# Two-layer hybrid decoder trunk: the buffers laid out anew in on-chip memory

## The chip, the cores and the metric

The kernel runs on one core of a Trainium2 chip. The core has five engines that run side by side and meet at semaphores: TensorE (matmuls, "PE" in the profile, its weight loads "PEld"), VectorE ("DVE"), ScalarE ("ACT"), GpSimd ("POOL") and SyncE ("SP"), which here issues all transfers between the main memory (HBM) and the on-chip memory (SBUF). SBUF has 128 partitions; a buffer is a range of bytes that starts at the same address in each of them. Matmuls write to a second memory, PSUM. The metric is the device time of one execution in microseconds.

## What is computed

Two layers over 256 tokens of width 1024, in float32. Each has a mixer (stick-breaking attention and softmax attention with rotary, 8 heads of 64 each, gated and merged) and a SwiGLU part of inner width 2816, each followed by a LayerNorm over alpha x plus the part's output:

```python
for l in range(DEPTH):                                        # DEPTH = 2
    proj = x @ w_in[l]                                        # 1024 -> 5120
    q_sb, k_sb, v_sb, q_mb, k_mb, v_mb, g_sb, g_mb = jnp.split(proj, cuts, axis=-1)
    o_sb = stick_breaking_attention(heads(q_sb, 8), heads(k_sb, 8), heads(v_sb, 8))
    o_mb = moba_attention(partial_rope(heads(q_mb, 8), pos), partial_rope(heads(k_mb, 8), pos), heads(v_mb, 8))
    merged = jax.nn.sigmoid(g_sb) * (merge_heads(o_sb) @ w_branch_sb[l]) \
           + jax.nn.sigmoid(g_mb) * (merge_heads(o_mb) @ w_branch_moba[l])
    x = layer_norm(ALPHA * x + merged @ w_out[l], ln_mix_g[l], ln_mix_b[l])
    ffn = (jax.nn.silu(x @ w_ffn_gate[l]) * (x @ w_ffn_up[l])) @ w_ffn_down[l]
    x = layer_norm(ALPHA * x + ffn, ln_ffn_g[l], ln_ffn_b[l])
```

## The kernel before

**Numbers in two parts.** Every operand of a matmul is held as two float32r parts, hi (rounded) and lo (the rest). A product a b is three matmuls, hi hi, hi lo and lo hi (`mm3`, whose matmuls all stand at line 275 in `mm`). A matmul has a stationary operand, 128 columns that a weight load puts into the array, and a moving operand that streams past it.

**Weights** come in 244 granules of 128 partitions x 1024 float32 (`WeightStream`): a load of 512 KB from SP into one of four buffers `raw` (L119), a cast by ScalarE into `whi` (helper line L48), and a subtraction by VectorE into `wlo` (L53). There are ten buffers each of whi and wlo; a granule's split starts when a pair is free. `Weave` writes one program order for all engines, in which these splits and the attention, rotary and norm steps stand between the matmuls of the main line.

**The stages of a layer** and their names in the profile: `pv`, `pq` (in layer 1 together `pvq`), `pk`, `pu` are projections with tokens on the partitions (`tok_major`): xT is stationary and 512 weight columns move. `pqk` (q and k of stick-breaking, four tiles of 2 x 24 matmuls), `pg` (gates, 8 x 48) and `pf` (SwiGLU from the fifth chunk on, 18 x 48) are feature-major (`feat_major`): 128 weight columns are stationary and all 256 tokens of xT move. `pb` is the branch projection with the attention's outputs `osb` and `omb` moving, `pw` the output projection, `pft` the first SwiGLU chunks in tok_major, `pd` the down projection (512 weight columns move, the activations `h` are stationary); in layer 1 its second half of tokens is `pe`, partly with 256 columns.

**xT** is the transposed x, in two parts xT_hi and xT_lo of 8 KB per partition; each norm writes it anew. x itself is `xs`, two tiles of 4 KB.

**Buffers** come from pools, laid one behind the other in SBUF in the order in which the pools are opened: `const`, `wpool` (raw, whi, wlo), `acts` (15 units of 4 KB), `work` (attention and small activations), `small`. Tiles of a few bytes take 32.

Of the kernel before, what the change touches and what calls it, by code (L numbers as in the profile page):

```python
# [7 lines left out]
F32 = mybir.dt.float32  # L8
F32R = mybir.dt.float32r
# [5 lines left out]
P = 128  # L15
DEPTH = 2
D = 1024
S = 256
KC = D // P
# [15 lines left out]
class Weave:  # L35
    """Program order: the main line of projections, with side lines (attention, norms,
    rotary, weight splits) woven in. Every engine takes its instructions in program order,
    so each is emitted about when its operands are there, by an estimate of the time at
    which each engine gets through what it has been given. A side line yields the time
    at which it goes on; on the tensor engine's clock."""  # L40

# [40 lines left out]
    def start(self, gen):  # L82
        """A side line whose first stage comes now."""
        side = self.add(gen)
        if not self.busy:
            self._step(side)
        return side
# [9 lines left out]
class WeightStream:  # L97
    """Weight granules [128, 1024]: loaded in float32, then split exactly into
    two float32r parts (hi = rounded, lo = the rest) for the tensor engine."""

# [24 lines left out]
    def line(self):  # L125
        """The side line: a granule at a time, as far as the buffers allow."""
        nc, weave = self.nc, self.weave
        while self.split < self.total:
            g = self.split
            ahead = g - self.current  # L130
            if g > self.limit:
                yield weave.t + 0.1
                continue
            if ahead >= LEAD and max(weave.dve_t, weave.act_t) > weave.t + BACKLOG:
                yield weave.t + 0.2
                continue
            self.load(g + NRAW)
            if ahead > 0:
                yield self.there[g]
            hi, lo = (self.pool.tile([P, GCOLS], F32R, tag=n, name=f"{n}{g}", bufs=NSPLIT)  # L140
                      for n in ("whi", "wlo"))
            t = self.raw.pop(g)
            n = GCOLS // len(self._pieces(g))
            for sl in self._pieces(g):
                e = weave.act(self.there[g], n, nc.scalar.copy, hi[:, sl], t[:, sl])
            if g - self.current > 0:
                yield e
            for sl in self._pieces(g):
                e = weave.dve(e, n, nc.vector.tensor_sub, lo[:, sl], t[:, sl], hi[:, sl].bitcast(F32))
            self.parts[g], self.ready[g] = (hi, lo), e  # L150
            self.split += 1
            self.load(g + 1 + NRAW)

    def allow(self, g):
        """Granule g's buffers are free from here on."""
        self.limit = max(self.limit, min(g, self.total - 1))
# [7 lines left out]


NRAW = 4
NSPLIT = 10
# [12 lines left out]
def hybrid_trunk_kernel(ctx: ExitStack, tc: tile.TileContext, w, xT_in, x_in, ln_in,  # L180
                        ident_in, mask_in, rope_in, out):
    nc = tc.nc

    const = ctx.enter_context(tc.tile_pool(name="const", bufs=1))
    wpool = ctx.enter_context(tc.tile_pool(name="wpool", bufs=1))
    acts = ctx.enter_context(tc.tile_pool(name="acts", bufs=15))
    work = ctx.enter_context(tc.tile_pool(name="work", bufs=3))
    small = ctx.enter_context(tc.tile_pool(name="small", bufs=2))
    psM = ctx.enter_context(tc.tile_pool(name="psM", bufs=2, space=PSUM))
# [22 lines left out]

# [1 line left out]
    xT_raw = [unit(f"xT_raw{t}", [P, KC, P]) for t in range(2)]  # L214
    ident = const.tile([P, P], F32, name="ident")
    rope = const.tile([P, 2, 2, ROPE], F32, name="rope")
    xs = [const.tile([P, D], F32, name=f"x{t}") for t in range(2)]
    xT_hi = const.tile([P, KC, S], F32R, name="xT_hi")
    xT_lo = const.tile([P, KC, S], F32R, name="xT_lo")
    mask = const.tile([P, 2, P], F32, name="mask")  # L220
# [4 lines left out]
    nc.vector.memset(zero, 0.0)  # L225
    nc.vector.memset(mhalf, -0.5)
    nc.scalar.activation(warm, zero, AF.Sigmoid)
    # The tensor engine's clock rises after some microseconds of work: give it zeros meanwhile.
    idle = unit("idle", [P, 512], F32R)
# [42 lines left out]

# [1 line left out]
    def mm(o, a, b, start, stop):  # L274
# [30 lines left out]
    def tok_major(o, g, t, first, last, k0):  # L305
        """o[tokens of t, 512] += x @ granule g ([2 kc, 512])."""
        hi, lo = ws.take(g)
        hi = hi.rearrange("p (k c) -> p k c", k=2)
        lo = lo.rearrange("p (k c) -> p k c", k=2)
        for k in range(2):  # L310
            ts = slice(t * P, (t + 1) * P)
            mm3(o, xT_hi[:, k0 + k, ts], xT_lo[:, k0 + k, ts], hi[:, k, :], lo[:, k, :],
                first and k == 0, last and k == 1)

    def both_tokens(name, g0, put):
        """All tokens of x @ granules g0..g0+3; put(tokens, bank) takes each half."""
        acc = [bankM(f"{name}{t}", [P, WIDTH]) for t in range(2)]
        order = ((0, 0), (1, 0), (0, 1), (1, 1), (0, 2), (0, 3)) if g0 == 0 else \
            ((0, 0), (0, 1), (0, 2), (1, 0), (1, 1), (0, 3))
        for t, k in order + ((1, 2), (1, 3)):  # L320
            tok_major(acc[t], g0 + k, t, k == 0, k == 3, 2 * k)
            if t == 1:
                ws.allow(g0 + k + NSPLIT)
            if k == 3:
                put(t, acc[t])

    def feat_major(o, g):
        """o[128 columns, 256 tokens] = (x @ granule g)^T, g [8 kc, 128 columns]."""
        hi, lo = ws.take(g)
        hi = hi.rearrange("p (k c) -> p k c", k=KC)  # L330
# [5 lines left out]
    def token_out(o, g, t, s_hi, s_lo, first, last):  # L336
        """o[tokens of t, 1024] += s^T @ granule g ([1 kc, 1024]); o: (first column, bank) ..."""
        hi, lo = ws.take(g)
# [6 lines left out]

    # Per head, q is stacked as [hi; lo] over the 128 rows and each part of k is there twice,
    # so that q k^T = q_stack (k_hi twice) + q_stack (k_lo twice).
    def stack_q(qs, src, n, c, e):
        """qs[head] [128, ...] from src [2 heads x 64, ...]; the second head is [lo; hi]."""
        for h, (a, b) in enumerate(ROWS):  # L350
# [20 lines left out]
    def rope_line(name, ps, t, put):  # L371
        """Token-major q or k (8 heads x 64) -> rotary -> transposed, handed to put."""
        tmp = work.tile([P, 8, DH], F32, tag="T", name=f"{name}_tok{t}")
# [22 lines left out]
    def scores(s, q, kh, kl, m):  # L396
        """Scores of both heads of a pair: columns 0:128 = (q0, k0), 128:384 = (q1, k0 k1),
        with the causal mask m added to the diagonal blocks."""
        for h in range(2):
# [12 lines left out]
    def weighted(name, p, wt, v, oT, e):  # L412
        """oT[:, p] = (wt @ v)^T for both heads of pair p."""
        yield e + MARGIN
# [93 lines left out]
    def scale_shift(e, x, cols, sub, op, scale, g, b, e_scale):  # L508
        """x <- ((x op sub) g) scale + b; yields each piece of columns as it is done."""
        for c in cols:  # L510
# [7 lines left out]
    def norm_line(name, t, junk, gb):  # L518
        """x_t <- LN(alpha x_t + ps) g + b, and its transpose into xT (split)."""
        x = xs[t]  # L520
# [26 lines left out]
    def last_norm(name, t, banks, gb, down):  # L547
        """The output's tokens: LN(alpha x_t + sum) g + b, blocks of columns in turn."""
        x = xs[t]
# [24 lines left out]

# [1 line left out]
    norms = []  # L576
    for l in range(DEPTH):
        G = l * NG_LAYER
        L = f"l{l}"

        # v of stick-breaking and q of MoBA: tokens 0..127 first
        v_sb = pair_tiles(L + "vsb", [P, 2, WIDTH])
# [28 lines left out]

        # Each pair of stick-breaking heads starts with its q and k; k and v of MoBA and the
        # first gates come between, MoBA's heads after the last sigmoid of stick-breaking, and
        # the gates' sigmoids after the last exponential of MoBA.
        o_sb = pair_tiles(L + "osb", [P, NPAIR, S])
# [47 lines left out]

        # branch projections and the gated merge, feature-major
        gb = load_gb(l, 0)
# [20 lines left out]

        # output projection: tokens 0..127 first
        norms = []
# [7 lines left out]

        # SwiGLU, first chunks token-major (tokens 0..127 first)
        h_t = [pair_tiles(f"{L}h{i}", [P, 4, S]) for i in range((NFC + 3) // 4)]
# [47 lines left out]

        # down projection: the last granules' tokens 0..127 first
        gb = load_gb(l, 1)
# [108 lines left out]
```

## Time and profile before

| | us |
|---|---|
| time, median of 3 runs (753.32 to 755.79) | 753.6 |
| span of the profiled execution | 747.6 |
| TensorE busy (98% of the span) | 735.1 |
| VectorE busy | 529.9 |
| ScalarE busy | 421.8 |
| GpSimd busy | 13.4 |

The span reaches from the first to the last instruction of the profiled execution; the median is 6.0 us longer than it. TensorE's busy time counts overlapping matmuls once, so it tells that matmuls follow each other nearly always, and not how fast. Transfers move 136.31 MB at a mean of 182 GB/s. The pace of the matmuls is read from the chain of work: the length of an unbroken piece, divided by the matmuls in it.

### The profile page before, as it was taken

What the parts mean: (1) busy time and instruction counts of PE and PEld (TensorE: products, weight loads), DVE (VectorE), ACT (ScalarE), POOL (GpSimd) and SP (SyncE); (2) the same over time, 40 slices, a digit from 0 to 9 for tenths busy, and PEclk for the clock granted to TensorE, in tenths of its full rate; (3) what the DMA queues carried; (4) which work ended last, traced back from release to release, by engine and by line L of the source; (5) the groups of instructions that cost most, each with busy time, mean ns of one, the idle gap of its engine ahead of it and who ended that gap; (6) DMA issues with size and microseconds to landing.
All of it is one profiled execution on the core that took longest, in us unless ns stands there. A gap on an engine that the chain in (4) does not pass through costs nothing.

```text
span 747.6 us, 12689 instructions
## 1 busy us (share of the span) xinstructions
PE 735.1 (98%) x5049; PEld 675.5 (90%) x5049; DVE 529.9 (71%) x772; ACT 421.8 (56%) x655; POOL 13.4 (2%) x20
## 2 busy tenths in 40 slices
PE   8999999999999999999999999999999999999996
PEld 5888999998799999988888889999987999999885
DVE  6897878696886666644488878886768866665416
ACT  6788867744565445433267877777435654554300
POOL 0000000000000000000000000000010000000001
PEclk9999999999999999999999999999999999999999
DMA  8864724554586565676168445345635865657501
GB/s 292 284 217 151 221 93 153 176 199 167 178 265 227 181 194 182 198 241 194 60 196 258 146 162 177 108 145 198 210 113 183 277 201 194 196 185 246 166 1 56
DMA packets 39082, 136.31 MB, mean 182 GB/s; under 512 B 4464, under 2 KB 6000, under 8 KB 39024
## 3 DMA queue, kind: packets, MB, share of 16 engines
q1 hardware_dynamic: 39024, 135.51, 55.6%
q8 instruction: 39, 0.64, 0.3%
q14 instruction: 19, 0.16, 0.1%
HBM read 134.45 MB, written 1.05 MB: 181 GB/s over the span
## 4 chain that ended last, share of the span: by engine, by line
PE 84%; DVE 6%; ACT 3%; DMA 3%; issue 2%; POOL 1%; SPq 0%; POOLq 0%; DVEq 0%; ACTq 0%
PE l0pf L275 14%; PE l1pf L275 13%; PE l0pd L275 8%; PE l1pg L275 6%; PE l0pg L275 6%; PE l1pe L275 4%; PE l1pd L275 4%; PE l1pb L275 3%; PE l0pb L275 3%; PE l1pvq L275 3%; DMA raw<-in_w_dram 3%; PE l1pw L275 2%; PE l0pw L275 2%; PE l1pqk L275 2%; DVE wlo L53 2%
## 5 line engine op out<-in xcount | busy, mean ns | idle before, releaser
L53 DVE TENSOR_TENSOR wlo<-raw,whi 128x1024 fp32r<-128x1024 f32 (+1 forms) x245 | 296.8, 1219 | 93.0 <-ACT whi L48 89.5
L48 ACT CAST whi<-raw 128x1024 fp32r<-128x1024 f32 (+1 forms) x245 | 254.1, 1046 | 86.7 <-PE l0pd L275 22.6
L275 PE MATMUL l0pf<-xT_hi,whi 128*128 128x256 f32 x288 | 81.0, 281 | 0.0
L275 PE MATMUL l0pf<-xT_lo,whi 128*128 128x256 f32 x288 | 80.9, 281 | 0.0
L275 PE MATMUL l0pf<-xT_hi,wlo 128*128 128x256 f32 x288 | 80.9, 281 | 0.0
L275 PE MATMUL l1pf<-xT_hi,whi 128*128 128x256 f32 x288 | 79.6, 276 | 0.0
L275 PE MATMUL l1pf<-xT_lo,whi 128*128 128x256 f32 x288 | 79.5, 276 | 0.0
L275 PE MATMUL l1pf<-xT_hi,wlo 128*128 128x256 f32 x288 | 79.5, 276 | 0.0
L275 PEld LDWEIGHTS l0pf<-xT_hi,wlo 128*128 128x128 f32 x288 | 55.3, 192 | 0.0
L275 PEld LDWEIGHTS l0pf<-xT_lo,whi 128*128 128x128 f32 x288 | 54.1, 188 | 0.0
L275 PEld LDWEIGHTS l1pf<-xT_lo,whi 128*128 128x128 f32 x288 | 54.1, 188 | 0.0
L275 PEld LDWEIGHTS l0pf<-xT_hi,whi 128*128 128x128 f32 x288 | 54.1, 188 | 0.0
L275 PEld LDWEIGHTS l1pf<-xT_hi,whi 128*128 128x128 f32 x288 | 54.1, 188 | 0.0
L275 PEld LDWEIGHTS l1pf<-xT_hi,wlo 128*128 128x128 f32 x288 | 54.1, 188 | 0.0
L275 PE MATMUL l0pg<-xT_hi,whi 128*128 128x256 f32 x128 | 35.9, 281 | 0.0
L275 PE MATMUL l1pg<-xT_hi,whi 128*128 128x256 f32 x128 | 35.9, 281 | 0.0
L275 PE MATMUL l0pg<-xT_lo,whi 128*128 128x256 f32 x128 | 35.5, 277 | 0.0
L275 PE MATMUL l1pg<-xT_lo,whi 128*128 128x256 f32 x128 | 35.5, 277 | 0.0
L275 PE MATMUL l1pg<-xT_hi,wlo 128*128 128x256 f32 x128 | 35.4, 277 | 0.0
L275 PE MATMUL l0pg<-xT_hi,wlo 128*128 128x256 f32 x128 | 35.4, 277 | 0.0
L275 PE MATMUL l0pd<-whi,l0h_hi 128*128 128x512 f32 x88 | 34.4, 391 | 0.0
L275 PE MATMUL l0pd<-whi,l0h_lo 128*128 128x512 f32 x88 | 34.3, 389 | 0.0
(379 smaller groups left out, 1821.1 us busy)
## 6 DMA issues: line engine op xcount, KB each, us to landing
raw<-in_w_dram SPq DMA_DIRECT2D x243, 512.0 KB, 4.1
ln<-in_ln_dram SPq DMA_DIRECT2D x8, 512.0 KB, 7.3
xT_raw<-in_xT_dram SPq DMA_DIRECT2D x8, 128.0 KB, 5.0
x<-in_x_dram SPq DMA_DIRECT2D x2, 512.0 KB, 6.4
out_dram<-x SPq DMA_DIRECT2D x3, 256.0 KB, 2.1
raw<-in_w_dram SPq DMA_DIRECT2D x2, 256.0 KB, 3.7
out_dram<-x SPq DMA_DIRECT2D x2, 128.0 KB, 2.0
mask<-in_mask_dram SPq DMA_DIRECT2D x1, 128.0 KB, 3.2
```

Source lines behind the costliest of these rows:

```text
L48: f(*args, **kw)
L53: f(*args, **kw)
L275: nc.tensor.matmul(o, a, b, start=start, stop=stop)
```

## The change

The pools are opened in another order, and a filler stands behind the small tiles. `const` keeps ident, rope, mask and the two constants; behind it come `small` and a pool `fill` with one tile `page` of 576 bytes; then `big` with xs, xT_hi and xT_lo; then wpool, acts and work as before. `page` has to be written once, so GpSimd sets one element of it. Comments and docstrings became blank lines.

```diff
+FILL = 144
@@
     const = ctx.enter_context(tc.tile_pool(name="const", bufs=1))
+    small = ctx.enter_context(tc.tile_pool(name="small", bufs=2))
+    fill = ctx.enter_context(tc.tile_pool(name="fill", bufs=1))
+    big = ctx.enter_context(tc.tile_pool(name="big", bufs=1))
     wpool = ctx.enter_context(tc.tile_pool(name="wpool", bufs=1))
     acts = ctx.enter_context(tc.tile_pool(name="acts", bufs=15))
     work = ctx.enter_context(tc.tile_pool(name="work", bufs=3))
-    small = ctx.enter_context(tc.tile_pool(name="small", bufs=2))
@@
-    xs = [const.tile([P, D], F32, name=f"x{t}") for t in range(2)]
-    xT_hi = const.tile([P, KC, S], F32R, name="xT_hi")
-    xT_lo = const.tile([P, KC, S], F32R, name="xT_lo")
+    xs = [big.tile([P, D], F32, name=f"x{t}") for t in range(2)]
+    xT_hi = big.tile([P, KC, S], F32R, name="xT_hi")
+    xT_lo = big.tile([P, KC, S], F32R, name="xT_lo")
+    page = fill.tile([P, FILL], F32, name="page")
@@
     nc.vector.memset(mhalf, -0.5)
+    nc.gpsimd.memset(page[:, :1], 0.0)
     nc.scalar.activation(warm, zero, AF.Sigmoid)
```

The built programs place the buffers so. The first 16,512 bytes are taken by the system and its constants in both; before, x0 starts at 16,512 + 512 (ident) + 256 (rope) = 17,280, and after, the small tiles and the filler end at 20,480, where x0 starts.

| buffers | first address before | offset modulo 512 before | first address after | offset modulo 512 after |
|---|---|---|---|---|
| ident, rope | 16,512 | 128 | 16,512 | 128 |
| x0, x1 | 17,280 | 384 | 20,480 | 0 |
| xT_hi, xT_lo | 25,472 | 384 | 28,672 | 0 |
| raw (4), whi (10), wlo (10) | 42,944 | 448 | 45,056 | 0 |
| units: v, q and k of MoBA, osb, omb, gates, m, h, ln | 141,248 | 448 | 143,360 | 0 |
| work: q and k of stick-breaking, ph, pl, T | 202,688 | 448 | 204,800 | 0 |

All sizes from x0 on are multiples of 1024 bytes, so the offset holds for each buffer of a row. Between a weight's start and xT's lie, modulo 512, 64 bytes before and none after; all other pairs of weights and activations keep a difference of 0.

With buffer numbers left out, the instructions of TensorE, VectorE, ScalarE and SP stand in the same order with the same waits. GpSimd has one more. Its first instructions in the program before, from the system's constants to the first norm:

```order
L843 MEMSET const-uint8-127 128x1
L853 UNCONDITIONAL_BRANCH
L58 ISA
L58 TENSOR_SCALAR l0a_ve_2113<-l0a_ve_2113 128x1
L58 TENSOR_TENSOR l0a_ve_2113<-l0a_ve_2113,mhalf 128x1
```

And the same place in the changed program:

```order
L850 MEMSET const-uint8-127 128x1
L860 UNCONDITIONAL_BRANCH
L233 MEMSET page 128x1
L58 ISA
L58 TENSOR_SCALAR l0a_ve_2121<-l0a_ve_2121 128x1
L58 TENSOR_TENSOR l0a_ve_2121<-l0a_ve_2121,mhalf 128x1
```

Only the memset of `page` came in; nothing on GpSimd stands ahead of it but the system's own start.

## Rows read from the trace of the kernel before

**Rows 1.** The page's first part: busy time, share of the span, instructions of each engine.
```profile
PE 735.1 (98%) x5049; PEld 675.5 (90%) x5049; DVE 529.9 (71%) x772; ACT 421.8 (56%) x655; POOL 13.4 (2%) x20
```

**Rows 2.** The page's fourth part: the chain that ended last, by engine.
```profile
PE 84%; DVE 6%; ACT 3%; DMA 3%; issue 2%; POOL 1%; SPq 0%; POOLq 0%; DVEq 0%; ACTq 0%
```

**Rows 3.** That chain in order of time: start us, length us, what, instructions.
```profile
4.47 5.78 DMA raw<-in_w_dram
10.55 4.64 DMA raw<-in_w_dram
...
77.56 5.44 PE l0pg L275 x48
...
83.92 5.65 PE l0pqk L275 x48
...
99.30 2.83 PE l0pg L275 x24
...
143.10 23.02 PE l0pb L275 x192
...
209.47 3.44 PE l0pft L275 x15
...
215.20 99.64 PE l0pf L275 x846
314.84 55.08 PE l0pd L275 x243
...
583.38 95.90 PE l1pf L275 x846
```

**Rows 4.** Busy time by stretch: stretch, length, engines with instructions, PEclk, DMA share, GB/s.
```profile
143.10:166.12 23.02, 23.02 (x194) 23.02 (x193) 18.89 (x30) 13.95 (x22) 0.00 (x0) 1.00 0.62 221
215.20:314.84 99.64, 99.64 (x847) 99.64 (x847) 66.05 (x90) 50.50 (x72) 0.00 (x0) 1.00 0.62 203
...
583.38:679.28 95.90, 95.90 (x848) 95.90 (x847) 65.88 (x90) 50.52 (x72) 0.00 (x0) 1.00 0.65 210
```

**Rows 5.** Groups of weight loads: line engine op names shapes xcount | busy us, mean ns.
```profile
L275 PEld LDWEIGHTS l1pf<-xT_hi,wlo 128*128 128x128 f32 x288 | 54.1, 188 | 0.0
...
L275 PEld LDWEIGHTS l0pb<-l0omb_hi,whi 128*128 128x128 f32 x32 | 6.1, 192 | 0.0
```

**Rows 6.** TensorE in time, entry of l0pb and 256 columns of l1pe: start, length.
```profile
142.94 0.28 PE L275 MATMUL l0pb<-l0osb_hi,whi 128*128 128x256 f32 x1
...
143.17 0.28 PE L275 MATMUL l0pb<-l0osb_hi,wlo 128*128 128x256 f32 x1
...
144.00 0.28 PE L275 MATMUL l0pb<-l0osb_hi,whi 128*128 128x256 f32 x1
...
144.36 0.28 PE L275 MATMUL l0pb<-l0omb_hi,whi 128*128 128x256 f32 x1
...
734.73 0.28 PE L275 MATMUL l1pe<-whi,l1h_hi 128*128 128x256 f32 x1
...
735.09 0.28 PE L275 MATMUL l1pe<-whi,l1h_hi 128*128 128x256 f32 x1
```

**Rows 7.** TensorE in time, start of the long stretch of l1pf.
```profile
583.34 0.28 PE L275 MATMUL l1pf<-xT_lo,whi 128*128 128x256 f32 x1
...
583.69 0.28 PE L275 MATMUL l1pf<-xT_lo,whi 128*128 128x256 f32 x1
...
584.49 0.28 PE L275 MATMUL l1pf<-xT_hi,wlo 128*128 128x256 f32 x1
```

**Rows 8.** Groups on GpSimd: xcount | busy us, mean ns | idle before us, releaser.
```profile
L58 POOL TENSOR_SCALAR l0a_ve<-l0a_ve 128x1 f32<-128x1 f32 x2 | 1.5, 748 | 190.0 <-ACT l0pw L48 190.0
...
L843 POOL MEMSET const-float32-0.0<- 128x1 f32 x1 | 0.1, 99 | 0.2 <-issue 0.2
```

**Rows 9.** Groups on VectorE: two steps of a norm on x.
```profile
L53 DVE SCALAR_TENSOR_TENSOR x<-x,l0a_ve,ln 128x512 f32<-128x512 f32 x4 | 2.8, 749 | 0.9 <-POOL l0a_ve L58 0.9
...
L53 DVE SCALAR_TENSOR_TENSOR x<-x,l0pw 128x512 f32<-128x512 f32 x4 | 2.6, 683 | 2.8 <-PE l0pw L275 2.8
```

## The prediction, made before the changed kernel ran

> **What bounds the kernel now.** The first view is the table of engines: TensorE is busy for 735.1 us, 98% of the span of 747.6 [rows 1]. That number alone proves little, because matmuls overlap in the pipeline. The second view, the chain that ended last, settles it: 84% of the span lies on TensorE, 6% on VectorE, 3% on ScalarE and 3% on transfers [rows 2]. So from about 62 us on the time is the number of matmuls multiplied by the pace at which they follow each other. Only the first 62 us, and 410 to 430 us in layer 1, hang on the supply of split weights.
>
> The third view is the same chain in order of time, because it gives that pace: the length of an unbroken piece divided by its matmuls. The reader should see that equal instructions (stationary 128x128, moving 128x256) run at three different paces. A gate piece has 48 in 5.44 us, which is 113.3 ns each; a piece of q and k of stick-breaking has 48 in 5.65 us, 117.7 ns; the branch projection l0pb has 192 in 23.02 us, 119.9 ns [rows 3]. SwiGLU's feature-major part runs at 117.8 ns in layer 0 (99.64 us for 846) and at 113.4 ns in layer 1 (95.90 us for 846) [rows 3]. Matmuls of 512 columns take 226.7 ns in l0pd (55.08 us for 243) and 229.3 ns in l0pft (3.44 us for 15) [rows 3].
>
> These are not waits for another engine. In l0pb and in both SwiGLU stretches TensorE and its weight loads are busy without a gap, the granted clock is 1.00 (the 2.4 GHz level), and VectorE is busy for 18.89 of 23.02, 66.05 of 99.64 and 65.88 of 95.90 us [rows 4]. What shows is a longer weight load: 192 ns in l0pb, 188 ns in l1pf [rows 5].
>
> **Which addresses go with which pace.** Take where a buffer starts in its partition, modulo 512 bytes (the table in the section on the change). All slices that TensorE reads begin a multiple of 512 bytes into their buffer, so they have their buffer's offset. Before, whi, wlo, the activations and the attention's tiles have 448, and xT_hi and xT_lo have 384. In l0pb and in the 256-column matmuls of l1pe both operands have 448; these run at 120. In pf, pg and pqk the stationary operand has 448 and the moving one 384; these run at 113 or 118.
>
> How a stretch gets to its pace says more than the pace. The first two steps of l0pb take 0.23 us together, from 142.94 to 143.17; from 144.00 on three take 0.36, and the average over all 192 is 119.9 [rows 3, 6]. So it settles at 120 and stays; in l1pe, behind 512-column matmuls, three steps from 734.73 take 0.36 as well [rows 6]. With xT it goes the other way: three steps from 583.34 take 0.35 us, and from 583.69 to 584.49 seven take 0.80, which is 114 [rows 7]. So I read 120 as the resting pace of the pair 448 and 448, and 113 or 118 as those of 448 and 384. The sizes fit one cause. Between 256 and 512 columns of l0pb's and l0pd's class lie 226.7 - 119.9 = 106.8 ns, so one 4-byte column passes per cycle of 2.4 GHz; 113.3 and 119.9 ns are 272 and 288 cycles, and the 16 cycles between them are 64 bytes, just what xT's offset differs by from that of the weights. That the next weight load and the running matmul collide when they read from equal offsets is an inference; the trace has only these two classes of 256-column pairs.
>
> **The change part by part.** It adds one memset of one element on GpSimd, ahead of everything that engine does later; the like takes 99 ns, and the next real work there waits 190.0 us [rows 8]. It costs nothing. The instructions of the other four engines and their semaphores stay as they are. The filler is 576 bytes and no transfer touches it. What is left is the offsets: 448 becomes 0, and 384 becomes 0. The difference between weights and activations stays zero, and **the one between xT and the weights goes from 64 bytes to zero**. So the matmuls that read xT move into the class of l0pb, and I price them with its pace, 119.9:
> - l0pf: 864 matmuls x (119.9 - 117.8) = 1.8 us.
> - l1pf: 864 x (119.9 - 113.4) = 5.6 us.
> - pg: of 384 per layer one piece of 24 is at 117.9 (2.83 us) [rows 3] and the rest at 113.3: 24 x 2.0 + 360 x 6.6 = 2.4 us, twice 4.9.
> - pqk: four tiles of 48 per layer, one at 117.7 and the others at about 113.3. The first two of layer 0 and the second of layer 1 stand beside weight splits that end later, so they cost nothing as long as that cover stays (at most 48 x 6.6 = 0.3 us each without it). The rest: 0.4 in layer 0 and 0.7 in layer 1, together 1.2 us after rounding.
>
> All of these lie on the chain, and VectorE, the next busiest, has slack in the long stretches [rows 4], so they add up: 13.5 us.
>
> The 512-column matmuls with xT as the stationary operand (576: v, q, k, u and pft) go the other way, since theirs also becomes the class of equal offsets, and that pair rests at 226.7 and not 229.3: 576 x 2.6 = 1.5 us less. About half of them stand in the stretches that the weight supply bounds, so I take 0.7 and keep 0 and 1.5 as ends.
>
> Transfers into raw change their target's offset from 448 to 0. Every transfer of before has an odd offset, so no row prices it. Where it would show is the start, whose chain has four loads of 4.64 to 5.78 us [rows 3]; their spread of 1.1 us is the nearest bound on both sides, and I take 0. By the Trainium skill's page DMA: Bandwidth & Descriptors, section How a descriptor splits into AXI transactions, a run that doesn't begin at a multiple of 256 bytes pays for one more transaction; for 4 KB that is 17 in place of 16, an estimate of 6% or 1.2 us over those loads, and the sum would be 11.6 in place of 12.8. No run here shows it yet.
>
> VectorE's and ScalarE's splits keep equal offsets among raw, whi and wlo, so they stay. The norms' steps on x with ln change from a difference of 64 to none; they take 749 ns against 683 ns with a PSUM operand [rows 9]. If all of these 66 ns went, or came on top, at some four steps on each of three norms' paths, that would be 0.8 us either way; I take 0.
>
> Sum: 13.5 - 0.7 = +12.8 us. The profiled span is 747.6 us, the median 753.6; the 6.0 us outside the span are not touched. Span 760.4, **time 766.4 us**. Bounds of this case: if the stretches now at 113 only go to 117.8, the gain in pace is 864 x 4.4 + 720 x 4.5 + 144 x 4.4 = 7.7 us, so 761; with no gain at 512 columns and a bad transfer 769.
>
> **The rivals.** First, **faster**: not the relation between the streams decides, but each buffer's own place. Then 448 as the moving operand's offset is what costs 16 cycles, 384 costs less, and 0 costs no more than 384. All 256-column matmuls would run at 113.4 or below: l0pf 864 x 4.4 = 3.8 us, pb 384 x 6.5 = 2.5, l1pe some 130 x 5 = 0.7, the pieces of pqk and pg at 118 0.6, 512 columns 0.7 to 1.5. That is 8.5 us less, 745.1 us. It decides from the point where a matmul with both operands at 0 takes less than 117 ns. Against it: 512-column moving operands have 448 in both of their classes, and those still differ (226.7 and 229.3), slower with the stationary at 384; and l0pb's first steps are faster than its pace later [rows 6], as with two streams that fall into step and not as with a read that is dearer each time. For it: the trace has no buffer at 0, so nothing excludes that such a start is better than all that it shows.
>
> Second, **no change**: the paces are phases into which TensorE falls by what stands before a stretch. For it, l0pf and l1pf have the same offsets and yet run at 117.8 and 113.4. Then 753.6 stays, unless a long stretch flips, which is 3.8 us. Against it, no 256-column stretch of l0pb's class rests at 113. The page SBUF — State Buffer of the Trainium skill, section Who interferes with whom, speaks for this rival: it gives TensorE two independent read ports, one for moving data and one for weight loads, and says that it never waits on anyone. By that rule the sum would be 0 and not 12.8; rows 5 and 3 agree poorly, since equal weight loads take 188 and 192 ns and equal matmuls three paces.
>
> That the change doesn't do what it says is out: in the built program all named buffers start at multiples of 4096 bytes.
>
> **How the numbers follow.** My forecast 0.60, the faster rival 0.20, no change 0.20. Time 766.4. The range takes in the forecast's bounds (761 to 769) and no change, and some of the faster rival where only part of it comes: 748 to 769; beyond it lies most of the faster rival. A measurement of this kernel tells about 0.3%, that is 2.3 us, from no change. Faster by more 0.20, within 0.20, slower 0.60.
>
> **What will show it.** Right: l1pf's stretch at about 120 ns per matmul, 101.5 us in place of 95.90, l0pf the same, gate pieces of 48 in 5.75 us, xT's weight loads at 192 ns, pb and pd as before, pft nearer 227. The first rival shows as pb below 119 and l0pf at 113. The second shows as unchanged pieces. A shorter start with shorter loads would show the transfer term. Wrong at the root would be pf at 113 beside pb at 120: then something other than the offsets parts these classes.

## The result, and the profile after

| | before | after |
|---|---|---|
| time, median of 4 executions each | 753.83 us | 762.22 us |
| lowest to highest | 753.32 to 755.79 | 761.99 to 762.57 |
| span of the profiled execution | 747.6 us | 760.4 us |

The ratio is 1.0116, with an interval of 1.0094 to 1.0138: the changed kernel is slower, by 1.2%. The span grew by 12.8 us, as forecast to the tenth, and the median by only 8.4. Both numbers need an explanation, and the first is in part luck.

The page of the changed kernel, its table of engines, which answers to [rows 1]:

```profile
PE 747.8 (98%) x5049; PEld 689.4 (91%) x5049; DVE 529.9 (70%) x772; ACT 421.4 (55%) x655; POOL 13.5 (2%) x21
```

TensorE has the same 5049 matmuls and is busy for 12.7 us more; VectorE is busy for the same time and ScalarE for 0.4 us less. The chain that ended last, changed kernel, in order of time (start us, length us, what, instructions), against [rows 3]:

```profile
78.72 5.76 PE l0pg L282 x48
...
85.40 5.76 PE l0pqk L282 x48
...
101.18 2.88 PE l0pg L282 x24
...
146.40 23.04 PE l0pb L282 x192
...
212.72 3.45 PE l0pft L282 x15
...
218.55 101.52 PE l0pf L282 x846
320.06 55.11 PE l0pd L282 x243
...
590.64 101.53 PE l1pf L282 x846
```

The long 256-column pieces with xT now have one pace: 5.76 / 48, 2.88 / 24 and 101.52 / 846 are all 120.0 ns. Layer 0's SwiGLU stretch is 1.88 us longer, layer 1's 5.63. The pieces that do not read xT, l0pb and l0pd, kept theirs within 0.03 us.

Busy time by stretch, changed kernel, both SwiGLU stretches (columns as in [rows 4]):

```profile
218.55:320.06 101.51, 101.51 (x847) 101.51 (x847) 65.84 (x90) 50.48 (x72) 0.00 (x0) 1.00 0.57 198
...
590.64:692.17 101.53, 101.53 (x848) 101.53 (x847) 65.95 (x90) 50.48 (x72) 0.00 (x0) 1.00 0.57 199
```

The granted clock is 1.00 as before, TensorE is busy through both stretches, and VectorE has as much work as before: no other engine holds TensorE up, its matmuls follow each other more slowly. The groups of weight loads, changed kernel, against [rows 5]:

```profile
L282 PEld LDWEIGHTS l1pf<-xT_hi,wlo 128*128 128x128 f32 x288 | 55.3, 192 | 0.0
...
L282 PEld LDWEIGHTS l0pb<-l0omb_hi,whi 128*128 128x128 f32 x32 | 6.1, 192 | 0.0
```

The load that took 188 ns in l1pf takes 192, the figure of l0pb's class. It was not that class's alone, though: in the kernel before, one of the three loads of l0pf, at 117.8 ns per matmul, took 192 as well.

```profile
L275 PEld LDWEIGHTS l0pf<-xT_hi,wlo 128*128 128x128 f32 x288 | 55.3, 192 | 0.0
```

TensorE in time at the start of l1pf, changed kernel, against [rows 7]:

```profile
590.60 0.29 PE L282 MATMUL l1pf<-xT_lo,whi 128*128 128x256 f32 x1
...
591.81 0.28 PE L282 MATMUL l1pf<-xT_hi,wlo 128*128 128x256 f32 x1
```

From 590.60 to 591.81 lie ten steps in 1.21 us. Before, the stretch came down from about 117 to 114 ns within ten steps; now it is at about 120 from its start.

### The profile page after: what moved, and what is told of

It is laid out like the page before. It is cut to its first block, busy times and chain, and to the rows that moved or that the text cites. A ratio compares the mean times of both kernels' runs of the same rounds, so it can differ in the third digit from the quotient of the medians.

```text
span 760.4 us, 12690 instructions
## 1 busy us (share of the span) xinstructions
PE 747.8 (98%) x5049; PEld 689.4 (91%) x5049; DVE 529.9 (70%) x772; ACT 421.4 (55%) x655; POOL 13.5 (2%) x21
## 3 DMA queue, kind: packets, MB, share of 16 engines
q1 hardware_dynamic: 39024, 135.51, 52.1%
## 4 chain that ended last, share of the span: by engine, by line
PE 86%; ACT 4%; DVE 4%; DMA 2%; issue 2%; POOL 1%; SPq 0%; POOLq 0%; DVEq 0%; ACTq 0%
PE l1pf L282 14%; PE l0pf L282 14%; PE l0pd L282 8%; PE l1pg L282 6%; PE l0pg L282 6%; PE l1pe L282 4%; PE l1pd L282 4%; PE l1pb L282 3%; PE l0pb L282 3%; PE l1pvq L282 3%; PE l0pqk L282 2%; PE l1pqk L282 2%; PE l1pw L282 2%; PE l0pw L282 2%; ACT whi L48 2%
## 5 line engine op out<-in xcount | busy, mean ns | idle before, releaser
L282 PE MATMUL l1pf<-xT_hi,whi 128*128 128x256 f32 x288 | 81.6, 283 | 0.0
L282 PE MATMUL l1pf<-xT_hi,wlo 128*128 128x256 f32 x288 | 81.5, 283 | 0.0
L282 PE MATMUL l1pf<-xT_lo,whi 128*128 128x256 f32 x288 | 81.5, 283 | 0.0
L282 PE MATMUL l0pd<-wlo,l0h_hi 128*128 128x512 f32 x88 | 34.3, 389 | 0.0
```

The lines of the kernel that those rows point to most:

```text
L282: nc.tensor.matmul(o, a, b, start=start, stop=stop)
```

## The experiments

Theory: the difference between the addresses of what TensorE streams and of the weights it loads, modulo some number of bytes, sets the resting pace. Rivals: each buffer's own place sets it; or paces are phases that go their own way. Edits are against the changed kernel unless said otherwise. "Difference" is xT's start minus the weights' start; before it is -64 bytes, after 0. Fillers that are only touched by a one-element memset stand between buffers to shift them. The code shown leaves out these memsets, @@ marks a jump, and what stands behind a # is a remark.

### The kernel before once more: how its own times lie

No edit: the kernel before, as it is.

> The kernel before, unchanged, to see how its executions differ. The first profiled execution has a span of 747.6 us with l0pf at 117.8 ns per matmul and l1pf at 113.4, while the timed ones lie at 753.3 to 755.8. Theory: the pace of the long stretches with xT is not fixed by the program (two resting paces, 113.4 and 117.8, as each stretch falls into one of them), so that a usual execution has l1pf at 117.8 too: span 747.6 + 864 x 4.4 ns = 751.4, and 2.2 us outside the span as in the changed kernel's executions (762.57 against 760.4). Rival: the paces are always as in that trace, span 747.6, and 6 us lie outside it.

Measured: 754.0 us, ratio 1.0007 (0.997 to 1.0044). The profiled execution, with a span of 748.7 us, showed the same pair of paces as [rows 3]. The kernel before's chain again:

```profile
216.52 99.64 PE l0pf L275 x846
...
584.45 95.90 PE l1pf L275 x846
```

More telling are the spans of the eleven executions of the kernel before in this comparison, these four and the seven beside them. Four lie at 748.2 to 748.7 us, with times of 750.39 to 750.96; seven at 751.2 to 752.1, with times of 753.9 to 755.16. The time is 2.1 to 3.5 us above the span in each, and the granted clock is 0.995 to 0.997 in both groups. So the 6.0 us between the profiled span of 747.6 and the median of 753.6 do not all lie around the span. They are some 2.2 us around it and 3.8 between two kinds of execution. In this comparison the two kinds lie 3.2 us apart on average; one SwiGLU stretch of 864 matmuls gains 3.8 us between 117.8 and 113.4 ns. The profile in front was of the quicker kind. That the slower kind is the one with both stretches at 117.8 is inferred: the traces kept of the kernel before are both of the quicker one.

Which kind is the usual one isn't fixed either. The four times in the table of the result, 753.32 to 755.79, lie near those of the slower kind; their spans are not on record. In the three other comparisons below, the kernel before has spans of 747.6 to 753.0: 15 of 34 are at 748.9 or below, 14 at 751.5 or above and 5 between, and its median time is 750.88, 751.08 or 754.41. So the 8.4 us by which the median grew hold against the slower kind; against a median of 750.9, an estimate from these numbers, the change would cost 11.3 us.

### All buffers at 448: is it the place or the difference?

```diff
-FILL = 144
+FILL = 128
```

> The changed kernel with a filler 64 bytes shorter: x, xT, weights, activations and attention tiles all start at 448 modulo 512, none on a multiple of its size. Theory of equal offsets (the difference between the streams decides): as the changed kernel, 762 us, span 760, all 256-column matmuls at 120.0 ns, 512-column ones at 226.7. Rival, each buffer's own place decides: it would lie elsewhere, towards 754 or below, or any time other than 762 by more than 1.5 us.

Measured: 762.66 us, ratio 1.0131 (1.0098 to 1.0164), span 760.5. The chain with everything at offset 448, in order of time:

```profile
78.86 5.76 PE l0pg L282 x48
...
218.68 101.51 PE l0pf L282 x846
...
590.70 101.51 PE l1pf L282 x846
```

The weights, the activations and the attention's tiles stand exactly as modulo 512 before, only xT moved to join them, and every length shown is that of the changed kernel within 0.02 us. Between these two places, 0 and 448, a buffer's own place does nothing. The faster rival falls.

### xT 64 bytes lower than the weights

```diff
     xs = [big.tile([P, D], F32, name=f"x{t}") for t in range(2)]
+    gap_x = big.tile([P, 112], F32, name="gap_x")
     xT_hi = big.tile([P, KC, S], F32R, name="xT_hi")
     xT_lo = big.tile([P, KC, S], F32R, name="xT_lo")
+    gap_w = big.tile([P, 16], F32, name="gap_w")
```

> The changed kernel with xT_hi and xT_lo alone moved by 448 bytes, so that they start 64 bytes before a multiple of 512 and everything else stays on its multiple. Theory of equal offsets: the difference of before is back, so the paces of before: pf and pg at 113.4 or 117.8, pb at 120, pft at 229; time 750 to 756, as the kernel before. Rival, own place of the weights: faster or equal paces than in the changed kernel only if xT's place matters; 762 if the weights' place at 0 is what costs.

Measured: 751.29 us (750.92 to 751.83), ratio 0.998 (0.9948 to 1.0013), span 748.6: the whole loss is gone, with weights, units and raw still at 0. The chain with the difference at -64:

```profile
144.06 23.02 PE l0pb L286 x192
...
216.13 95.91 PE l0pf L286 x846
...
580.76 99.64 PE l1pf L286 x846
```

The two SwiGLU stretches have changed places: 113.4 ns now in layer 0, 117.8 in layer 1. Which of the two paces a stretch takes is therefore not a property of the layer or of the difference; both belong to the difference of -64. That much of the rival "phases" is right. Its groups of weight loads tell the two paces apart:

```profile
L286 PEld LDWEIGHTS l1pf<-xT_hi,wlo 128*128 128x128 f32 x288 | 55.3, 192 | 0.0
L286 PEld LDWEIGHTS l1pf<-xT_lo,whi 128*128 128x128 f32 x288 | 54.1, 188 | 0.0
...
L286 PEld LDWEIGHTS l0pf<-xT_hi,wlo 128*128 128x128 f32 x288 | 54.1, 188 | 0.0
```

At 113.4 all loads take 188 ns; at 117.8 one of the three takes 192, here that of wlo; at 120 all take 192. Which of the three it is isn't fixed: in the second profile of the kernel before, with l0pf at 117.8 too, it is a load of whi, and wlo's takes 188.

```profile
L275 PEld LDWEIGHTS l0pf<-xT_hi,whi 128*128 128x128 f32 x288 | 55.3, 192 | 0.0
```

These times are a sign of the pace and not shown to be its cause.

### Other differences: 256, 64, 128, 32, -32, -96

All have the edit above with other sizes of the two gaps.

```diff
-    gap_x = big.tile([P, 112], F32, name="gap_x")   # the edit for -64
-    gap_w = big.tile([P, 16], F32, name="gap_w")
+    gap_x = big.tile([P, 64], F32, name="gap_x")    # +256; the other five below
+    gap_w = big.tile([P, 64], F32, name="gap_w")
```

The sizes of gap_x and gap_w are 16 and 112 for +64, 32 and 96 for +128, 8 and 120 for +32, 120 and 8 for -32, 104 and 24 for -96.

> The changed kernel with xT_hi and xT_lo alone at 256 modulo 512, all else at 0. Theory of equal offsets in its narrow form (only streams that start at the same place modulo 512 collide): no collision, pf and pg at 113.4 or less, about 749 us or below. If the period is shorter (128 or 256 bytes), 256 is again equal: 120 ns, 762 us. If the own place decides, a multiple of 256 is as good as one of 512: 762.

> The changed kernel with xT alone at 64 modulo 512, all else at 0. If the two streams collide when they stand on the same one of two alternating 64-byte pieces (period 128 bytes), +64 is the same as -64: pf and pg at 113.4 or 117.8, time 750 to 756. If the period is 256 bytes, +64 is a case of its own: 762 where a lag of 64 bytes the other way collides, else 751 or less. If only equal starts collide: 749 to 754.

> The changed kernel with xT alone at 128 modulo 512, all else at 0. Period of 128 bytes: equal to no difference, all at 120.0 and 226.7, 762 us. Period of 256 bytes: a case of its own, without a collision at the start, 749 to 754.

> The changed kernel with xT alone at 32 modulo 512, all else at 0, so that xT's rows begin in the middle of a 64-byte piece. If 64-byte pieces count, 32 is still the same piece as the weights' and stays slow: 256-column matmuls at 117 to 120, 757 to 763. If 32-byte pieces count: as a difference of 64, 750 to 755. If a stream that begins inside a piece pays for one more piece: above 763.

> The changed kernel with xT alone 32 bytes below a multiple of 512 (480). Below the weights 64 bytes gave 113.4 or 117.8, above them 32 gave 116.7 and 64 gave 117.8. If the sign of the difference decides: 113 to 117, 750 to 754. If only whole 64-byte pieces free the streams: 117 to 120, 755 to 762.

> The changed kernel with xT alone 96 bytes below a multiple of 512 (416). If any distance between 64 and 128 bytes below the weights keeps the streams apart: 113.4 to 117.8, 750 to 754. If distance works by whole 64-byte pieces only, it lies between the cases of -64 and +128 (118.7): 752 to 760.

Measured, with the mean ns per matmul worked out from the chain (the length of l0pf over 846; l1pf gives the same within 0.1 except at -64) and, in the last column, the mean over the three long pieces of l0pft (60 matmuls of 512 columns), which have xT stationary:

| difference, bytes | time us | ratio to before | pf, 256 columns | pft, 512 columns |
|---|---|---|---|---|
| 0 (after) | 762.22 | 1.0116 (1.0094 to 1.0138) | 120.0 | 229.0 |
| 256 | 763.09 | 1.0135 (1.0102 to 1.0169) | 120.0 | 228.3 |
| 128 | 760.36 | 1.0115 (1.0091 to 1.0138) | 118.7 | 232.7 |
| -96 | 759.78 | 1.0105 (1.0077 to 1.0133) | 118.7 | 233.5 |
| -32 | 759.54 | 1.0101 (1.0073 to 1.0129) | 118.3 | 233.2 |
| 64 | 757.95 | 1.0084 (1.0061 to 1.0108) | 117.8 | 233.8 |
| 32 | 755.70 | 1.0058 (1.0039 to 1.0077) | 116.7 | 232.8 |
| -64 (the run above) | 751.29 | 0.998 (0.9948 to 1.0013) | 113.4 and 117.8 | 229.7 |

The kernel before, with -64, has 229.7 in the last column. The ratios are not on one footing, since its own median was 753.83 us beside 0, 754.22 beside 256 and -64, 750.88 beside 128, 64 and 32, and 751.08 beside -96 and -32. The times and paces are what the rows are compared by.

The l0pf rows of the six chains, in the order 256, 64, 128, 32, -32, -96, and of the run with 64 also a piece of l0pft:

```profile
218.37 101.53 PE l0pf L286 x846
```

```profile
211.30 3.53 PE l0pft L286 x15
...
217.17 99.64 PE l0pf L286 x846
```

```profile
218.13 100.39 PE l0pf L286 x846
```

```profile
217.13 98.70 PE l0pf L286 x846
```

```profile
217.90 100.11 PE l0pf L286 x846
```

```profile
217.81 100.40 PE l0pf L286 x846
```

256 bytes act as 0 in time and in pace, and 128 does not. That fits a pace that repeats every 256 bytes; no other pair that lies 256 apart was run. Nothing is symmetric: in its profile +64 rests at 117.8 in both layers and in neither at 113.4, and +32 is quicker than -32. Of the eight, -64, the kernel before's own, is the quickest. There are more than two resting paces, so "equal offsets collide, unequal ones do not" was too simple. Differences other than 0 and 256 also make the 512-column matmuls slower.

The time of a weight load does not go with the pace at these differences. At +64, with 117.8 ns, the three groups of l0pf take 187 to 188 ns, and none has the 192 that goes with 117.8 at -64:

```profile
L286 PEld LDWEIGHTS l0pf<-xT_hi,wlo 128*128 128x128 f32 x288 | 53.9, 187 | 0.0
```

### The activations 64 bytes lower instead of xT

```diff
     wpool = ctx.enter_context(tc.tile_pool(name="wpool", bufs=1))
+    ugap = ctx.enter_context(tc.tile_pool(name="ugap", bufs=1))   # one tile [P, 112]
     acts = ctx.enter_context(tc.tile_pool(name="acts", bufs=15))
```

> The changed kernel with only the units and the attention's tiles moved by 448 bytes, so that osb, omb, m and h lie 64 bytes below the weights' offset, and xT stays equal to the weights. Theory of equal offsets: pf and pg stay at 120.0, but pb goes to 113.4 or 117.8 (192 x 2.2 to 6.6 ns = 0.4 to 1.3 us less per layer), l1pe's 256-column matmuls go to about 114 (132 x 4 = 0.5 us less), and pd and pw, 512 columns, from 226.7 to about 229 (some 590 x 2.5 = 1.5 us more): within 1.5 us of 762. If it is xT's tensor itself and not the difference of offsets, pb stays at 120.

Measured: 760.14 us, ratio 1.0108 (1.008 to 1.0136), span 758.5. The chain with the activations at -64:

```profile
147.12 21.78 PE l0pb L285 x192
...
218.12 101.52 PE l0pf L285 x846
319.63 55.62 PE l0pd L285 x243
```

And its groups of weight loads:

```profile
L285 PEld LDWEIGHTS l0pf<-xT_hi,whi 128*128 128x128 f32 x288 | 55.3, 192 | 0.0
...
L285 PEld LDWEIGHTS l0pb<-l0omb_hi,whi 128*128 128x128 f32 x32 | 6.0, 188 | 0.0
```

The classes are exchanged: l0pb now runs at 113.4 ns and loads in 188, and l0pf stays at 120. So the effect is not xT's own: a second pair of buffers shows it. l0pd's 512-column matmuls went from 226.8 to 228.9 ns.

### Both lower: the best that the classes promise

```diff
-FILL = 144
+FILL = 128
@@
     wpool = ctx.enter_context(tc.tile_pool(name="wpool", bufs=1))
+    ugap = ctx.enter_context(tc.tile_pool(name="ugap", bufs=1))
@@
+    gap_w = big.tile([P, 16], F32, name="gap_w")    # behind xT_lo: weights at 0, xT at 448
+    gap_u = ugap.tile([P, 112], F32, name="gap_u")  # units and work at 448
```

> Weights at 0, and xT, units and attention tiles all 64 bytes below that (448): the difference that gave 113.4 and 117.8, now for xT, osb, omb, m and h alike. Theory of equal offsets: pf, pg, pqk as in the kernel before, pb at 113.4 (384 x 6.6 ns = 2.5 us less than before), l1pe's 256 columns at 113.3 (132 x 5.9 = 0.8 less), pw and pd at 229 (some 590 x 2 = 1.2 us more): about 2 us below the kernel before. If the gains of the two moves do not add, 751 to 755.

Measured: 752.92 us over 12 executions against 751.08 over 17 of the kernel before, ratio 1.0011 (0.9994 to 1.0029), span 750.0: no gain, where 2 us were expected. The chain with both at -64:

```profile
143.70 21.76 PE l0pb L287 x192
...
214.62 99.64 PE l0pf L287 x846
314.26 55.64 PE l0pd L287 x243
...
582.18 99.64 PE l1pf L287 x846
```

The gain at l0pb came (1.26 us against [rows 3]), and l1pb has it too. What took it back against the quicker kind of the kernel before: both SwiGLU stretches rest at 117.8, where that has one at 113.4, and l0pd is 0.56 us longer. Some gate pieces took the slower pace as well. A piece of l0pg in the kernel before, at 113.6 ns:

```profile
90.59 3.75 PE l0pg L275 x33
```

And here, at 118.2:

```profile
90.84 3.90 PE l0pg L287 x33
```

This is also the trace that shows both stretches at 117.8 at the difference of -64.

### Only the low weights shifted: which streams meet?

```diff
     wpool = ctx.enter_context(tc.tile_pool(name="wpool", bufs=1))      # raw, whi
+    gap1 = ctx.enter_context(tc.tile_pool(name="gap1", bufs=1))        # one tile [P, 16]
+    wlpool = ctx.enter_context(tc.tile_pool(name="wlpool", bufs=1))    # wlo
+    gap2 = ctx.enter_context(tc.tile_pool(name="gap2", bufs=1))        # one tile [P, 112]
```

> The changed kernel with wlo alone 64 bytes above a multiple of 512; raw, whi, xT and all else at 0. It tells which pair of streams meets. In a feature-major product the matmuls run in threes: whi with xT_hi, whi with xT_lo, wlo with xT_hi. If the running matmul meets the weight load of the next one, the second of the three runs beside a load of wlo that is 64 bytes apart, so the step from the second to the third is the short one (113 to 118) and the other two are long (up to 120). If a matmul meets its own weights' place, the step after the third is the short one. Mean over pf 116 to 119 either way, 755 to 761 us. If what counts is the whole program's layout and no pair, all three steps are alike.

Measured: 759.88 us, ratio 1.0077 (1.0052 to 1.0101), span 758.5. The chain with wlo alone at +64:

```profile
146.31 22.61 PE l0pb L290 x192
...
218.57 99.65 PE l0pf L290 x846
318.23 56.38 PE l0pd L290 x243
```

Of each triple of matmuls two have a difference of 0 (with whi) and one of -64 (with wlo). If each matmul had its own pair's pace, or that of its neighbour's load, two of the three would stand at 120 and one apart. TensorE in time, one triple of l0pf, same run:

```profile
250.22 0.28 PE L290 MATMUL l0pf<-xT_hi,whi 128*128 128x256 f32 x1
250.34 0.28 PE L290 MATMUL l0pf<-xT_lo,whi 128*128 128x256 f32 x1
250.46 0.28 PE L290 MATMUL l0pf<-xT_hi,wlo 128*128 128x256 f32 x1
250.58 0.28 PE L290 MATMUL l0pf<-xT_hi,whi 128*128 128x256 f32 x1
```

Three equal steps of 0.12 us; over the stretch the means of the three are 117.4, 117.6 and 118.3 ns. In the kernel before's l0pf, where all three have a difference of -64, they are 117.6, 117.3 and 118.3: one pair in three at -64 is enough for that pace. So the pace belongs to the sequence and not to one pair, and which two streams meet stays open. The edit also puts whi and wlo 64 bytes apart from each other, and no run parts that from the rest. The 512-column matmuls pay for it: l0pd takes 232.0 ns each, where it took 226.8.

## Why the prediction was right, and where it was off

**The classes: right.** That the difference between xT and the weights, and not the clock or another engine, parts the paces was the root of the sum. With the place ruled out at 448, the loss taken back by -64 and the classes exchanged by moving the activations, this is shown. The collision behind it, which the prediction called an inference, remains one, and as it put it, of a weight load with the running matmul at equal offsets, it does not explain the paces at other differences. Its reckoning that 16 cycles are just the 64 bytes of the difference doesn't hold either: 64 bytes the other way give 117.8 ns, which is 5 cycles less than 120.0, and 128 bytes give 118.7, 3 less.

**The term of l0pf** was 1.8 us and measured 1.88. **The term of l1pf** was 5.6 and measured 5.63 between the two profiled executions. But this is the step that was mis-sized for the median. If in the executions that were timed both stretches stood at 117.8 (inferred above), l1pf lost 1.8 us there and not 5.6. The prediction saw that two equal stretches had unlike paces and used that for a rival; it did not ask how often the quick one occurs.

**The step to the median failed in the same place.** "The 6.0 us outside the span are not touched" added them to the new span. All four executions of the changed kernel lie only 2.1 to 2.4 us above their spans (762.57 against 760.4). With 12.8 - 3.8 = 9.0 us on 753.6, the 3.8 being inferred, the forecast would have been 762.6, and 762.2 was measured.

**pg and pqk** were put at 4.9 and 1.2 us. All pieces of l0pg on the chain, 384 matmuls, take 43.89 us before and 45.98 after, those of l1pg 43.89 and 45.99: 4.2 us in both layers. The prediction's mix of paces has a mean of 113.6 ns before; it was 114.3, because short pieces between the attention's matmuls are slower, as this one of before at 114.4:

```profile
96.32 2.06 PE l0pg L275 x18
```

After, the mean is 119.7. The pieces of pqk that the prediction priced lost 0.35 us in layer 0, and in layer 1 all of pqk lost 0.60: 1.0 us and not 1.2.

**The 512-column gain** of 0.7 us came, in good part. In layer 1 the pieces of pvq, pk, pu and pft on the chain took 48.70 us and now take 48.09. Of these 0.6 us, 0.3 lie in pk, where one piece of six took 272 ns per matmul before and so held a wait. In layer 0, pu and pft gained 0.07 us; from l0pb's end to l0pf's start lie 49.08 us before and 49.11 after. The sign that was named, pft nearer 227, is weak: over both layers its mean went from 229.6 to 228.4 ns.

**The start** was later, and the sum had no term for that. The first pieces of l0pu begin at 63.16 us, where before they began at 62.17. It is not the change's: in the second profile of the kernel before they begin at 63.46, and in the run with -64 at 62.87.

**So the span was hit in part by luck.** The priced terms came to 1.9 + 5.6 + 4.2 + 1.0 - 0.7 = 12.0 us where 12.8 were forecast, and 1.0 us of a later start filled the gap, less some 0.1 elsewhere. Against the second profile of the kernel before, 748.7 us, the span grew by 11.7.

**Transfers at zero: right.** The Trainium skill's page DMA: Bandwidth & Descriptors, section How a descriptor splits into AXI transactions, would have given an estimate of 1.2 us back with raw at a multiple of 256 bytes. In the changed kernel alone it looks as if transfers had become quicker: the DMA part of its profile page and the list of issues say

```profile
q1 hardware_dynamic: 39024, 135.51, 52.1%
...
raw<-in_w_dram SPq DMA_DIRECT2D x243, 512.0 KB, 3.7
```

where before had 55.6% and 4.1 us. But in the run with xT at -64, whose raw also starts at a multiple of 256, the same lines are

```profile
q1 hardware_dynamic: 39024, 135.51, 55.3%
...
raw<-in_w_dram SPq DMA_DIRECT2D x243, 512.0 KB, 4.1
```

and with all at 448 they have 54.7% and 4.2 us. Over the ten experiments with raw at such a multiple (all but the kernel before and the one at 448) the median landing is 4.0 to 4.1 us, against 4.1 to 4.2 in the three profiles with raw at 448. So that the 52.1% come from the new offset isn't shown, and nothing at the start became shorter.

**The rivals.** Faster by place: out. No change because paces are phases: wrong for this change, yet its observation, two paces at one difference, is what most likely separates 12.8 us from 8.4. The Trainium skill's page SBUF — State Buffer, section Who interferes with whom, with its two independent read ports and its TensorE that never waits, spoke for no change. The runs disagree: at a granted clock of 1.00 and with the same instructions on TensorE, xT 64 bytes lower changed l0pf from 101.52 to 95.91 us.

## What to carry to other kernels

Where a kernel is bound by back-to-back matmuls like these, the address difference between moving and stationary buffers, within 256 bytes, is worth testing like any other parameter: here rounding all buffers to the same boundary was the worst choice of those tried for 256 columns. Before adding an expected change to a median, check whether the profiled execution is of the usual kind; a median 6.0 us above the profiled span, where each execution's time lies 2.1 to 3.5 us above its own, was the sign. When a stretch can rest at two paces, price it at both and ask which is the common one.

## What the hardware showed that was not expected

- One difference can have two resting paces: at -64 a stretch of 864 equal matmuls settles at 113.4 or at 117.8 ns and keeps it to its end. Which one it takes changes with the layer and the program, and, as the spans suggest but no trace shows, with the execution.
- The pace depends on the difference, and not symmetrically: 120.0 ns at 0 and 256, 118.7 at 128 and -96, 118.3 at -32, 117.8 at 64, 116.7 at 32.
- 512-column matmuls with xT stationary rank the differences otherwise: 228 to 229 ns at 0 and 256, 229.7 at -64, 232.7 to 233.8 at the five others.
- A weight load's recorded time tells the pace only in part: at 0 and -64 it goes with it (188 ns at 113.4, 192 at 120.0), at +64 it is 187 to 188 ns at 117.8.
